# The last MLP's first matrix as seven block products, with weight sums made by adding DMAs

## The chip, the cores and the metric

The kernel runs on one core of a Trainium2 chip. The metric is the device time of one execution in microseconds; before the change the median of three runs is 2379.36 us (2377.18 to 2381.88).

## What is computed

A trunk of two layers on 1024 tokens of width 1024. Layer 0 is an mLSTM mixer and an MLP, layer 1 a latent attention mixer and an MLP. What matters here is the MLP, which both layers have:

```python
D_MODEL, SEQ, D_FF = 1024, 1024, 4096

def sqrelu_mlp(h, w1, w2):
    return jnp.square(jax.nn.relu(h @ w1)) @ w2

for l in range(DEPTH):
    ...
    x = x + g1[:, None, :] * rmsnorm(y, norm_g[l, 1])
    h = modulate(rmsnorm(x, norm_g[l, 2]), sh2, sc2)
    y = sqrelu_mlp(h, mlp_w1[l], mlp_w2[l])
    x = x + g2[:, None, :] * rmsnorm(y, norm_g[l, 3])
```

## The kernel before

**Halves.** The 1024 tokens are worked on as two halves of 512 (`hfs[0]`, `hfs[1]`). Activations lie with features on the 128 partitions and tokens along the free dimension, in 8 blocks of 128 x 512 for a half.

**Three matmuls for one product.** Each operand is split into a high part (fp32r) and the rest (low, fp32r), and `mm3` (L230 to L233) adds low x high, high x low and high x high. So a 128 x 128 block of weights against 512 tokens is three matmuls of 512 columns. A weight tile of 128 x 1024 is loaded by `wload` into one of four `raw` buffers (L211, SP's queue), and `wsplit` makes its two parts in the `ws` buffers, of which there are eight: a cast on ScalarE (L189) and a subtraction on VectorE (L190).

**The MLP.** `mlp` (L946) is a generator of steps. `hidden(f)` makes one block of 128 hidden features for 512 tokens: 8 blocks of D x 3 matmuls = 24 matmuls of 512 columns into one PSUM bank `ps`, then relu and square on ScalarE (L962, L963) and the split into high and low (L471, L472). `up_rows` and `up_cols` multiply a group of hidden blocks (4 in the last MLP) by a part of the second matrix, again 24 matmuls a step, and add the result to the output tiles (`accumulate`, L198). Hidden steps and up steps alternate: the ups of one group stand between the hidden steps of the next. Each step's weights are asked for two steps ahead (`AHEAD`, L944). There are four MLPs of 64 such steps: layer 0 half 0, layer 0 half 1, layer 1 half 0, layer 1 half 1, in this order.

**The order of the work.** Python generators are woven by hand. `two_streams` steps an MLP as the dense stream beside another stream (a mixer of the other half), and a filler. `go` ties the PE instructions of a step behind the last PE instruction before it; instructions of other engines are not tied by it, and each engine's order comes from a scheduler that takes an instruction when its operands and buffers are there. The first MLP (`f0`) runs beside a filler (`bg_latent`) that loads the adaLN weights (L352), makes the rotary tables (L1078 to L1102) and folds weights. The second and third MLPs run beside the mixers of layer 1. The last one runs beside `all_out`, which turns the residual stream into rows (`x_to_rows`, L1573 to L1579) and writes the output (`rows_out`, L1611 to L1623): the first half's in the middle of the last MLP, the second half's at its end.

**Norm before the MLP.** `post` adds the mixer's output to the residual, takes the norm and calls `normed`, which writes the split `h2`: 8 multiplications by gain and norm (L481) and 8 splits with a shift (L474 on ScalarE, L475 on VectorE).

**POOL.** GpSimd does little: nine small loads at the start (L264), the memset of the gate weights (L613), of the value tiles (L645, L648), small memsets that claim a buffer (L170), and in attention one memset for each even block (L1346).

Of the kernel before, what the change touches and what calls it, by code (L numbers as in the profile page):

```python
# [9 lines left out]
F32 = mybir.dt.float32  # L10
# [7 lines left out]
P = 128  # L18
# [64 lines left out]
def kernel(  # L83
# [39 lines left out]
    def k4v(dt=F32, b=512):  # L123
        return k4(dt)[:, :1024].rearrange("p (a b) -> p a b", b=b)
# [13 lines left out]
    def tmc(dt=F32):  # L138
        return sb.tile([P, 512], dt, tag="tmc", bufs=TMC, name=f"tmc_{next(uid)}")
# [42 lines left out]
    def paced():  # L182

        return tc.issue_after(pace[0]) if pace[0] else nullcontext()
# [42 lines left out]

    pe_last = [None]

    def mm3(o, lh, ll, rh, rl, start, stop):  # L230
        nc.tensor.matmul(o, ll, rh, start=start, stop=False)  # L231
        nc.tensor.matmul(o, lh, rl, start=False, stop=False)  # L232
        pe_last[0] = nc.tensor.matmul(o, lh, rh, start=False, stop=stop)  # L233


    nc.scalar.preload_act_table_set("natural_log_exp_and_others")
# [231 lines left out]
    def split_mod(hi, lo, u, sh):  # L468

        if sh is None:  # L470
            nc.scalar.copy(hi, u)  # L471
            nc.vector.tensor_sub(lo, u, hi.bitcast(F32))  # L472
        else:
            nc.scalar.activation(hi, u, AF.Identity, bias=sh)  # L474
            nc.vector.scalar_tensor_tensor(lo, u, sh, hi.bitcast(F32), ALU.add, ALU.subtract)  # L475

    def normed(h, xs_, rstd, A, sh):

        for k in range(KD):
            with paced():  # L480
                nc.vector.scalar_tensor_tensor(  # L481
                    xs_[k], xs_[k], A[:, k : k + 1], rstd, ALU.mult, ALU.mult
                )
                split_mod(h.hi[k], h.lo[k], xs_[k], sh[:, k : k + 1])
            if k % 4 == 3:
                yield 1

# [455 lines left out]
    NF = DFF // P  # L943
    AHEAD = 2  # L944

    def mlp(l, hf, y, sizes, rows=False):  # L946


        w1, w2, h = mlp_w1[l], mlp_w2[l], hf.h2
        hids = {}  # L950

        def hidden(f):
            def hid(w):
# [99 lines left out]
        for G in sizes:  # L1053
            fs = list(range(f0, f0 + G))
            f0, done = f0 + G, 0
            for i in range(G):
# [7 lines left out]
        for n in range(len(steps) + AHEAD):  # L1064
            if n < len(steps):
                ready.append(steps[n][0]())
            if n >= AHEAD:
                yield from steps[n - AHEAD][1](ready.pop(0))

                yield steps[(n - AHEAD + 1) % len(steps)][1].__name__  # L1070


    rope_d = scratch([2, P, S], "rope_d")
# [494 lines left out]

    def x_to_rows(half):

        for k in range(KD):
            a, b = tmc(), tmc()
            nc.sync.dma_start(a, xs_blk(k, half))  # L1573
            yield
            pt = pc()
            for t in range(4):
                nc.tensor.transpose(pt[:, ts(t, P)], a[:, ts(t, P)], ident)
            nc.scalar.copy(b, pt)
# [19 lines left out]
    def rows_out(hf, y, B):  # L1598

        xt = []  # L1600
        for t in range(4):
            a = k4v()
            r0 = hf.i * H + t * P
            nc.sync.dma_start(a, xr[r0 : r0 + P, :].rearrange("p (a b) -> p a b", b=512))
            xt.append(a)
        yield
        for t in range(4):
            yt, st = y.t[t], small(4)
            for g in range(2):
                junk = ps()  # L1610
                nc.scalar.activation(junk, yt[:, g], AF.Square, accum_out=st[:, g : g + 1])  # L1611
            ys = [tmc(), tmc()]
            v, r, w = small(1), small(1), small(1)
            with tc.high_priority(PRIO):
                for g in range(2):
                    nc.vector.tensor_mul(ys[g], yt[:, g], B[:, g])
                nc.vector.tensor_scalar(v, st[:, 0:1], st[:, 1:2], 1.0 / D, ALU.add, ALU.mult)
                nc.vector.tensor_scalar_add(v, v, EPS)
                rsqrt_(r, v, w)
            for g in range(2):  # L1620
                nc.vector.scalar_tensor_tensor(ys[g], ys[g], r, xt[t][:, g], ALU.mult, ALU.add)
                r0 = hf.i * H + t * P
                nc.sync.dma_start(out[0, r0 : r0 + P, ts(g, 512)], ys[g])  # L1623
            yield


# [126 lines left out]
    A1 = gain(2, NG(0, 2), adac(0, SC2))  # L1753
    B1 = gate(3, NG(0, 3), adac(0, G2))

    def post(hf, y, B, src, A, sh):
# [5 lines left out]
        yield 0  # L1762
        hf.h2 = Split()
        yield from normed(hf.h2, y, rstd, A, sh)

# [124 lines left out]
    drain(p1)  # L1890
    two_streams(f0, behind(bg_latent(), 4))
    rope_perm()


    z1 = FH(claim=True)
    ya = [None, None]

    def mixer1(hf, z, attention):
        att = attention(hf)
        lat = latent(hf, lambda: next(att))  # L1900
        next(lat)

        yield from to_x(hf, z)
        yield "fill"
        yield from lat
        yield next(att)
        yield from att
# [6 lines left out]
        yield from post(hf, y, B2, x_cols, A3, adac(1, SH2))  # L1914
# [5 lines left out]
    two_streams(mlp(1, hfs[0], u0, [2] * 16, True), mixer1(hfs[1], z1, attention_second))  # L1920
    u1 = FH(claim=True)

    def all_out():
        yield from x_to_rows(0)
# [43 lines left out]
```

## Time and profile before

| | |
|---|---|
| profiled execution | 2377.5 us |
| its span | 2375.5 us |
| median of the runs | 2379.36 us |
| granted TensorE clock, mean | 0.997 |
| instructions | 30534 |
| loads of MLP weights | 256 of 512 KB |

The page's times are of one execution. Matmuls are pipelined: a matmul's printed duration is longer than the distance to the next one's start, and the distance is what a row of matmuls costs. A group's line gives its count, its busy time, the mean duration in ns, then the idle time of the engine before it and what ended that. In a window's answer the columns are the busy times of PE, PEld (weight loads), DVE, ACT and POOL with their counts, the clock, the share of the DMA engines in use and GB/s.

### The profile page before, as it was taken

What the parts mean: (1) busy time and instruction counts of PE and PEld (TensorE: products, weight loads), DVE (VectorE), ACT (ScalarE), POOL (GpSimd) and SP (SyncE); (2) the same over time, 40 slices, a digit from 0 to 9 for tenths busy, and PEclk for the clock granted to TensorE, in tenths of its full rate; (3) what the DMA queues carried; (4) which work ended last, traced back from release to release, by engine and by line L of the source; (5) the groups of instructions that cost most, each with busy time, mean ns of one, the idle gap of its engine ahead of it and who ended that gap; (6) DMA issues with size and microseconds to landing.
All of it is one profiled execution on the core that took longest, in us unless ns stands there. A gap on an engine that the chain in (4) does not pass through costs nothing.

```text
span 2375.5 us, 30534 instructions
## 1 busy us (share of the span) xinstructions
PE 2343.4 (99%) x11621; PEld 1946.7 (82%) x11621; DVE 1549.6 (65%) x2435; ACT 1055.6 (44%) x1716; POOL 18.2 (1%) x93
## 2 busy tenths in 40 slices
PE   7999999999999999999999999999999999999998
PEld 5888888788888888888888888888888888888887
DVE  6667866868666667877764967765666486353345
ACT  4355334655333454434443554444444453444333
POOL 1000000000000000000000000000000000000000
PEclk9999999999999999999999999999999999999999
DMA  9452664544664745555543454874434354364431
GB/s 313 149 142 85 186 181 139 168 133 144 186 181 143 250 135 187 160 161 183 182 133 113 147 166 163 249 248 136 148 98 143 114 169 129 102 191 140 144 102 62
DMA packets 377106, 374.48 MB, mean 158 GB/s; under 512 B 24355, under 2 KB 282464, under 8 KB 376960
## 3 DMA queue, kind: packets, MB, share of 16 engines
q1 hardware_dynamic: 376672, 372.44, 50.3%
q8 instruction: 91, 1.49, 0.3%
q14 instruction: 55, 0.45, 0.1%
q0 software_dynamic: 288, 0.10, 0.0%
HBM read 313.24 MB, written 59.24 MB: 157 GB/s over the span
## 4 chain that ended last, share of the span: by engine, by line
PE 89%; DVE 4%; DMA 4%; ACT 1%; issue 1%; SPq 0%; DVEq 0%; ACTq 0%
PE ps L231 16%; PE ps L233 16%; PE ps L232 16%; PE pm L231 9%; PE pm L232 9%; PE pm L233 9%; PE pc L1450 1%; DMA raw<-in_a_w_in_dram 1%; DMA raw<-in_mlp_w_dram 1%; PE pc L231 1%; PE pc L233 1%; PE pc L232 1%; PE pm L1336 1%; DVE wl L190 1%; PE pm L820 1%
## 5 line engine op out<-in xcount | busy, mean ns | idle before, releaser
L190 DVE TENSOR_TENSOR wl<-raw,wh 128x1024 fp32r<-128x1024 f32 (+2 forms) x366 | 438.9, 1202 | 442.7 <-ACT wh L189 435.7
L189 ACT CAST wh<-raw 128x1024 fp32r<-128x1024 f32 (+2 forms) x366 | 377.6, 1035 | 704.3 <-PE ps L231 381.7
L231 PE MATMUL ps<-k,wl 128*128 128x512 f32 x1528 | 605.2, 396 | 2.5 <-ACT k L679 1.4
L233 PE MATMUL ps<-k,wh 128*128 128x512 f32 x1528 | 596.1, 390 | 0.0
L232 PE MATMUL ps<-k,wh 128*128 128x512 f32 x1528 | 595.6, 390 | 0.0
L231 PEld LDWEIGHTS ps<-k,wl 128*128 128x128 f32 x1528 | 287.0, 188 | 65.1 <-issue 2.9
L233 PEld LDWEIGHTS ps<-k,wh 128*128 128x128 f32 x1528 | 286.8, 188 | 61.7 <-issue 0.5
L232 PEld LDWEIGHTS ps<-k,wh 128*128 128x128 f32 x1528 | 287.2, 188 | 58.8 <-issue 1.7
L198 DVE TENSOR_TENSOR k<-k,pm 128x512 f32<-128x512 f32 (+1 forms) x254 | 211.0, 860 | 104.1 <-PE pm L233 103.6
L231 PE MATMUL pm<-hd,wl 128*128 128x512 f32 x512 | 200.9, 392 | 0.5 <-ACT hd L471 0.5
L232 PE MATMUL pm<-hd,wh 128*128 128x512 f32 x512 | 199.3, 390 | 0.2 <-DVE hd L472 0.2
L233 PE MATMUL pm<-hd,wh 128*128 128x512 f32 x512 | 199.2, 389 | 0.0
L231 PE MATMUL pm<-wh,hd 128*128 128x512 f32 x488 | 192.2, 394 | 1.6 <-ACT raw L1342 1.3
L232 PE MATMUL pm<-wl,hd 128*128 128x512 f32 x488 | 190.9, 391 | 0.0
L233 PE MATMUL pm<-wh,hd 128*128 128x512 f32 x488 | 190.2, 390 | 0.0
L359 DVE SCALAR_TENSOR_TENSOR tma<-raw,cond,tma 128x512 f32<-128x512 f32 x168 | 125.6, 748 | 20.4 <-DMA raw<-in_kv_ada_w_dram 14.4
L472 DVE TENSOR_TENSOR hd<-tmp,hd 128x512 fp32r<-128x512 f32 x128 | 88.3, 690 | 54.7 <-ACT hd L471 54.4
L1342 ACT ACTIVATE raw<-pm,sm 128x128 f32<-128x128 f32 (+3 forms) x64 | 47.5, 742 | 150.1 <-DVE sm L1341 121.8
L231 PEld LDWEIGHTS pm<-hd,wl 128*128 128x128 f32 x512 | 96.2, 188 | 20.8 <-ACT hd L471 0.9
L232 PEld LDWEIGHTS pm<-hd,wh 128*128 128x128 f32 x512 | 96.1, 188 | 20.5 <-DVE hd L472 0.5
L233 PEld LDWEIGHTS pm<-hd,wh 128*128 128x128 f32 x512 | 96.1, 188 | 20.2
L231 PEld LDWEIGHTS pm<-wh,hd 128*128 128x128 f32 x488 | 91.6, 188 | 22.3 <-ACT raw L1342 3.5
(354 smaller groups left out, 3426.2 us busy)
## 6 DMA issues: line engine op xcount, KB each, us to landing
raw<-in_mlp_w_dram SPq DMA_DIRECT2D x256, 512.0 KB, 4.2
raw<-in_ada_w_dram SPq DMA_DIRECT2D x80, 512.0 KB, 4.2
raw<-in_a_w_in_dram SPq DMA_DIRECT2D x48, 512.0 KB, 4.8
xs<-k SPq DMA_DIRECT2D x40, 256.0 KB, 4.8
raw<-in_kv_ada_w_dram SPq DMA_DIRECT2D x16, 512.0 KB, 4.0
raw<-in_a_w_out_dram SPq DMA_DIRECT2D x16, 512.0 KB, 4.8
kd<-k SPq DMA_DIRECT2D x32, 256.0 KB, 3.8
vd<-k SPq DMA_DIRECT2D x32, 256.0 KB, 4.5
```

The lines of the kernel that those rows point to most:

```text
L189: nc.scalar.copy(hi[:, :n], r[:, :n])
L190: i = nc.vector.tensor_sub(lo[:, :n], r[:, :n], hi[:, :n].bitcast(F32))
L198: return f(*a, **k)
L231: nc.tensor.matmul(o, ll, rh, start=start, stop=False)
L232: nc.tensor.matmul(o, lh, rl, start=False, stop=False)
L233: pe_last[0] = nc.tensor.matmul(o, lh, rh, start=False, stop=stop)
L359: nc.vector.scalar_tensor_tensor(acc, r[:, kk], cond[:, k : k + 1], acc, ALU.mult, ALU.add)
L472: nc.vector.tensor_sub(lo, u, hi.bitcast(F32))
L820: nc.tensor.matmul(nv[:, r, i], hf.PT[p_][:, r, cs], v[2 * p_ + r], start=g == 0, stop=True,)
L1336: nc.tensor.matmul(o[:, :w], qh, kh, start=False, stop=True)
L1342: nc.scalar.activation(pr[:, :n], f, AF.Exp, bias=m, scale=SCALE, accum_out=l)
L1450: nc.tensor.transpose(pt[:, ts(2 * e + i, P)], u.prs[i][:, ts(b + e, P)], ident)
```

## The change

The last MLP (layer 1, half 1) makes its hidden blocks in pairs. The 1024 rows of a pair's weights are cut in two (kh), its 256 hidden features in two (even, odd), the 512 tokens in two, and the four result blocks are made from seven block products of 512 x 128 x 256 in place of eight, by sums of operand blocks:

- **Operands of tokens.** `quarters` takes the place of the split `h2` for this half: seven quarter-size sums (`B[1]` to `B[7]`), each split into high and low. Four are made when the norm is, three at step 61 of the MLP before (`with_rest`).
- **Operands of weights.** `weight_sums` makes four sums for each of 16 pairs in a DRAM scratch `sums`: eight DMAs of 128 x 4 x 128 fp32 (256 KB) on POOL's queue, four that copy and four that add to what is there. One group of them is issued after each yield of the first MLP. The other three weight blocks are read from the weights as they are.
- **Steps.** A pair has four steps with 2, 2, 1 and 2 products of 12 matmuls of 256 columns. The banks go on accumulating after ScalarE or VectorE have taken a partial result (`more=True`). Up steps stand behind the first and the second. Loads are asked for three steps ahead.
- **Output.** `x_to_rows` loads the next block of x while it turns one; `rows_out` asks for x one row tile at first, then up to three; `all_out` goes one step at every second step of the MLP. The claim of `u1` is gone.

```diff
+    def weight_sums(w):
+        for p_ in range(NF // 2):
+            a = lambda f, kh: wcols(w, (2 * p_ + f) * P, P, 4 * kh, 4)
+            o = lambda i: by_k(sums[p_][:, ts(i, H)])
+            put = nc.gpsimd.dma_start
+            put(o(1), a(1, 0))
+            put(o(2), a(1, 0))
+            yield
+            put(o(1), a(0, 0), accum_op=ALU.add)
+            put(o(2), a(1, 1), accum_op=ALU.add)
+            yield
+            put(o(0), o(1))
+            yield
+            put(o(0), a(1, 1), accum_op=ALU.add)
+            yield
+            put(o(3), o(0))
+            yield
+            put(o(3), a(0, 1), accum_op=ALU.add)
+            yield
...
+            def product(i, o, w, start=False):
+                (wh, wl), (bh, bl) = w, B[i]
+                for k in range(4):
+                    mm3(o, wh[:, k], wl[:, k], bh[k], bl[k], start and k == 0, k == 3, more=not start)
...
+            def first(w):
+                u.b, u.x, u.s, u.r = cut(ps()), cut(pc()), tmp(), tmp()
+                product(1, u.b, w[0], True)
+                    nc.scalar.copy(u.s1, u.b)
+                product(2, u.x, w[1], True)
+                    nc.vector.tensor_add(c, u.s1, u.x)
+                    nc.scalar.activation(c, c, AF.Relu)
...
+            def second(w):
+                u.z = cut(pc())
+                product(6, u.b, w[0])
+                    nc.scalar.copy(u.s16, u.b)
+                product(7, u.z, w[1], True)
+                    nc.scalar.copy(u.s7, u.z)
...
+            def third(w):
+                u.w3 = w[1]
+                product(5, u.b, w[0])
+                    nc.vector.tensor_add(u.r[:, N:], u.s7, u.b)
...
+            def fourth(w):
+                product(4, u.z, w)
+                    nc.vector.tensor_add(cut(u.r), u.s16, u.z)
+                    nc.scalar.activation(u.r, u.r, AF.Relu, scale=-1.0)
+                    finish(2 * p_ + 1, u.r)
+                product(3, u.b, u.w3)
+                    nc.scalar.activation(u.s[:, N:], u.b, AF.Relu)
+                    finish(2 * p_, u.s)
...
+                (lambda: pieces(wload([(0, 0, wcols(w1, 2 * p_ * P))], P)), first),
+                (from_sums(0), second),
+                (from_sums(1), third),
+                (lambda: wload([(0, 0, wcols(w1, (2 * p_ + 1) * P, P, 4, 4))], P), fourth),
...
+            for i in range(0, G if B else 0, 2):
+                four = pair(fs[i] // 2)
+                for part in (four[:1], four[1:2], four[2:]):
+                    steps += part
+                    if part is not four[2:] and done < len(prev):
+                        steps.append(up(prev, done, False))
+                        done += 1
...
+        early = AHEAD + bool(B)
...
+    def with_weight_sums(g):
+        bg = weight_sums(mlp_w1[1])
+        for v in g:
+            next(bg, None)
+            yield v
+        drain(bg)
...
-    two_streams(f0, behind(bg_latent(), 4))
+    two_streams(with_weight_sums(f0), behind(bg_latent(), 4))
...
-    dense = mlp(1, hfs[1], u1, [4] * 8, True)
+    dense = mlp(1, hfs[1], u1, [4] * 8, True, B)
+    n = 0
     while (d := go(dense)) is not end:
-        if v != "last" and d != "within":
+        n += d != "within"
+        if v != "last" and d != "within" and n % 2:
             v = next(fill)
```

`finish` squares a hidden block on ScalarE and splits it, as the hidden step did.

More of the change, by code (lines that the diff above doesn't have):

```diff
@@ L1762, in post @@
         yield 0
+        if kept:
+            yield from kept(y, rstd)
+            return
         hf.h2 = Split()
@@ L1890, with quarters, part, rest @@
     drain(p1)
-    two_streams(f0, behind(bg_latent(), 4))
+    two_streams(with_weight_sums(f0), behind(bg_latent(), 4))
     rope_perm()
+    B = {}
+    later = [None]
+    def quarters(y, rstd):
+        q = lambda kh, th, j: y.t[2 * kh + j][:, :, ts(th, 256)]
+        sub = nc.vector.tensor_sub
+        def part(i, kh, th):
+            t = [k4v(F32R, 256), k4v(F32R, 256)]
+            for j in range(2):
+                s = ts(j, 2)
+                split_wide(t[0][:, s], t[1][:, s], q(kh, th, j))
+            B[i] = [[a[:, k] for k in range(4)] for a in t]
+        yield from normed_kept(y, rstd, A3, adac(1, SH2))
+        part(1, 0, 0)
+        part(2, 1, 0)
+        yield 1
+        minus = lambda o, a: nc.vector.scalar_tensor_tensor(
+            o, a, -1.0, o, ALU.mult, ALU.subtract
+        )
+        for j in range(2):
+            sub(q(0, 0, j), q(0, 0, j), q(0, 1, j))
+        part(3, 1, 1)
+        for j in range(2):
+            sub(q(0, 1, j), q(1, 1, j), q(0, 1, j))
+            minus(q(1, 1, j), q(0, 0, j))
+        part(6, 1, 1)
+        for j in range(2):
+            minus(q(1, 0, j), q(1, 1, j))
+        def rest():
+            part(7, 0, 1)
+            part(5, 0, 0)
+            part(4, 1, 0)
+        later[0] = rest
+        yield 1
     z1 = FH(claim=True)
@@ L1913, in mixer1, with with_rest @@
         yield 1
-        yield from post(hf, y, B2, x_cols, A3, adac(1, SH2))
+        yield from post(hf, y, B2, x_cols, A3, adac(1, SH2), quarters if hf.i else None)
     two_streams(mlp(0, hfs[1], z1, [2] * 14 + [4]), mixer1(hfs[0], z0, attention_first), bg_rest())
     u0 = FH(claim=True)
-    two_streams(mlp(1, hfs[0], u0, [2] * 16, True), mixer1(hfs[1], z1, attention_second))
-    u1 = FH(claim=True)
+    def with_rest(g):
+        n = 0
+        for v in g:
+            if v != "within":
+                n += 1
+                if n == 61:
+                    later[0]()
+            yield v
+    two_streams(
+        with_rest(mlp(1, hfs[0], u0, [2] * 16, True)), mixer1(hfs[1], z1, attention_second)
+    )
+    u1 = FH()
     def all_out():
```

97 lines of the change are left out of this document (78 added, 19 removed).

## The prediction

> **What bounds the kernel now.** I read the page's busy times and its chain first, then the windows, then single stages.
>
> ```profile
> PE 2343.4 (99%) x11621; PEld 1946.7 (82%) x11621; DVE 1549.6 (65%) x2435; ACT 1055.6 (44%) x1716; POOL 18.2 (1%) x93
> ...
> PE 89%; DVE 4%; DMA 4%; ACT 1%; issue 1%; SPq 0%; DVEq 0%; ACTq 0%
> ```
>
> TensorE is busy for 99% of the span and is 89% of the chain that ended last: only work taken from PE, or PE made to wait, can move the end. The windows (PE, PEld, DVE, ACT and POOL busy, clock, DMA share, GB/s) show where PE isn't full.
>
> ```profile
> 0.00:10.00 10.00, 3.17 (x10) 1.55 (x10) 3.99 (x21) 5.50 (x9) 6.21 (x22) 1.00 0.77 272
> 10.00:20.00 10.00, 8.43 (x45) 5.78 (x44) 5.86 (x12) 6.70 (x14) 0.00 (x0) 1.00 1.05 385
> 20.00:30.00 10.00, 6.12 (x28) 3.18 (x27) 7.52 (x14) 4.41 (x7) 0.00 (x0) 0.70 1.06 375
> 30.00:40.00 10.00, 10.00 (x54) 6.70 (x53) 8.39 (x14) 1.71 (x3) 0.00 (x0) 0.96 1.06 386
> ```
> ```profile
> 2010.87:2365.60 354.73, 354.73 (x1584) 292.65 (x1583) 154.02 (x217) 143.34 (x221) 0.00 (x0) 1.00 0.40 123
> ```
>
> The first 40 us are bound by loads: DMA share 1.05 at 385 GB/s, PE with gaps. The last MLP (2010.87 to 2365.6) is the other extreme: PE never idle, DVE 43%, ACT 40%, DMA 0.40. The change edits the second place; its weight sums may land in the first.
>
> **The products.** The MLP's first matrix today is 24 matmuls of 512 columns per hidden block of 128; the change makes it 84 of 256 columns for two blocks (7 products x 4 k x 3). The rate is the distance between starts, not the printed duration, since matmuls overlap. One hidden step, first matmul to the first of the next:
>
> ```profile
> 2010.87 0.39 PE L231 MATMUL ps<-k,wl 128*128 128x512 f32 x1
> ...
> 2016.31 0.39 PE L231 MATMUL ps<-k,wl 128*128 128x512 f32 x1
> ```
>
> 24 starts in 5.44 us: 0.2267 us each. For 256 columns with new weights each time, the value projection of layer 0:
>
> ```profile
> 303.48 0.28 PE L233 MATMUL ps<-wh,k 128*128 128x256 f32 x1
> ...
> 305.99 0.28 PE L233 MATMUL ps<-wh,k 128*128 128x256 f32 x1
> ```
>
> 21 starts (7 triples) in 2.51 us: 0.1195 us each, 5% more than half of 0.2267. Before: 32 x 24 x 0.2267 = 174.1 us. After: 16 x 84 x 0.1195 = 160.6 us. **-13.5 us**, not the eighth of 174 (21.8) that seven products for eight suggest. The Trainium skill (TensorE: Matmul & The Clock Gate, "Back-to-back issue gap") gives N/2.4 + 2.5 ns, an estimate of 109 ns for 256 columns and 216 for 512; by it the gain would be 19 us. The trace disagrees by 10 us per thousand matmuls at both sizes, and the trace is used.
>
> **What the products add.** Durations of the last MLP, then of 256-column forms elsewhere:
>
> ```profile
> L190 DVE TENSOR_TENSOR wl<-raw,wh 128x1024 fp32r<-128x1024 f32 x61 | 74.6, 1223 | 151.4 <-ACT wh L189 151.2
> ...
> L472 DVE TENSOR_TENSOR hd<-tmp,hd 128x512 fp32r<-128x512 f32 x32 | 22.1, 692 | 17.5 <-ACT hd L471 17.5
> ```
> ```profile
> L189 ACT CAST wh<-raw 128x1024 fp32r<-128x1024 f32 x61 | 64.3, 1054 | 169.9 <-PE ps L231 142.8 <-PE pm L232 27.1
> L963 ACT ACTIVATE tmp<-tmp 128x512 f32<-128x512 f32 x32 | 20.3, 635 | 1.0
> L471 ACT CAST hd<-tmp 128x512 fp32r<-128x512 f32 x32 | 19.8, 620 | 1.0
> L962 ACT ACTIVATE tmp<-ps 128x512 f32<-128x512 f32 x32 | 18.9, 590 | 0.0
> ```
> ```profile
> L1470 ACT COPY tmp<-ps 128x256 f32<-128x256 f32 x24 | 9.0, 373 | 11.5 <-PE ps L233 11.4
> ```
> ```profile
> L472 DVE TENSOR_TENSOR k<-ps,k 128x256 fp32r<-128x256 f32 x8 | 3.4, 421 | 0.8 <-ACT k L471 0.8
> ```
>
> - Load: a pair needs 3.5 loads of 512 KB in place of 2. DVE gets 24 more splits (29 us) and 48 adds of 0.42 (20): 203 of some 345 us. ACT gets 24 casts (25) and 48 copies of 0.37 (18): 187. DMA goes from 64 such loads to 88, share 0.40 to 0.55. None is near PE. The loads three ahead cover it: four raw tiles hold four steps. The one slot that comes late (the third step's second weights live until the fourth ends) makes an ACT cast wait, with the fourth step's relu and square behind it; they are needed a step of 24 x 0.1195 = 2.9 us later, so 0.
> - Waits of PE: product 3 goes into the bank that DVE has just added from; product 4 covers 12 x 0.1195 = 1.43 us. The add takes 0.42, and 1.64 if a weight split is ahead of it: 0 to 0.2 us, 16 times. I take **+1** of 0 to 3.4; the other banks have a whole second-matrix step between writer and reader.
> - The end: today an up step (5.4 us) stands between the last hidden step and the closing steps. After, the fourth step is followed by them at once. From product 3's end: relu 0.37, square 0.635, cast 0.62, subtract 0.69 = 2.3, and about 0.8 more because ACT is still on the odd block's three (1.85 us, begun 0.42 after product 4, against product 3's 1.43). The closing step's first six matmuls (1.36) use the earlier pair. **+2** (0 to 3).
> - New groups: seven per pair in place of two, 80 more group starts. No such row stands alone; 0 to 0.05 us each, **+1**.
>
> **The four-quarter operands.** Eight DVE operations of 0.75 go, 14 splits and 8 sums come: about +9 us on DVE, +9 on ACT, in the MLP before.
>
> ```profile
> L475 DVE SCALAR_TENSOR_TENSOR k<-k,ada,k x8: 748/751/753, 1953.3 to 1965.8; 128x512 fp32r<-128x512 f32 x8
> ```
>
> The old operands were ready at 1966.5, and PE came to them at 2010.87: 44 us of cover. The last three quarters are made at step 61 of 64, 16 us before the end of that MLP, and product 7 comes third. Cost 0; if that cover were gone, 9. The output steps of the first half go at every second step, and their loads of x move on SP's queue from four at once to one, then two: behind them stand weight loads. Of 24 k4 tiles the quarters hold 14, two results 8, a gain 1, so one is free, and an x load can keep SP until DVE has finished a tile's rows. The weight load behind it is three steps early, so 0 (to 3). The memset claim dropped on POOL costs and gains nothing.
>
> **The weight sums.** 128 DMAs of 256 KB on POOL's queue, half copies, half adding, 33.5 MB written. No row shows an adding DMA, or one from DRAM to DRAM. What POOL pays to issue, and the nearest transfers:
>
> ```profile
> L264 POOL DMA_DIRECT2D raw<-in_ada_b_dram x2 | 1.1, 542 | 0.0
> L264 POOL DMA_DIRECT2D raw<-in_norm_g_dram x1 | 0.7, 705 | 0.3 <-issue 0.3
> ...
> L264 POOL DMA_DIRECT2D raw<-in_a_gate_b_dram x1 | 0.5, 502 | 0.0
> ```
> ```profile
> DMA packets 66022, 61.62 MB, mean 175 GB/s; under 512 B 4048, under 2 KB 54736, under 8 KB 66001
> ...
> q1 hardware_dynamic: 66001, 61.35, 56.4%
> ```
>
> Two rows of data cost 0.50 us to issue, 64 rows of 512 bytes 0.70: 3.3 ns per row, so 512 runs cost between 0.5 and 2.2 us. All 128: 64 to 282 us of POOL, which is otherwise busy for 18. In the first MLP (512 to 865 us, the second fence) 61.35 MB took 56.4% of 353 us, 308 GB/s; 33.5 MB are 109 us at that rate, up to twice that if adding reads the old sum as well. Spread there the share becomes 0.87 to 1.18, with loads two steps (10.9 us) ahead. So where do they run? They wait for nothing but each other. What the trace does with such work:
>
> ```profile
> L1078 SPq DMA_DIRECT2D inv<-in_inv_freq_dram x4: 311/699/2118, 28.8 to 34.2; - x4
> ```
> ```profile
> L1081 DVE MEMSET sg<- x4: 59/59/59, 2.4 to 2.7; 32x1 f32 x4
> ```
> ```profile
> L1085 SPq DMA_DIRECT2D tmc<-in_positions_dram x2: 420/497/574, 538.8 to 572.5; - x2
> ```
>
> All three are written in the filler of the first MLP. The third needs a shared buffer and runs there; the first two need none and run in the first 35 us. The sums' DRAM has no other user either, so at least their first copies can start at some 7 us, in the stretch bound by loads. Against a large price: six of a pair's eight wait for an earlier one of the pair to land, and after 40 us PE is full and loads have slack. I take **+2** in the forecast (0 to 5), and the rest as rivals.
>
> **Sum.** -13.5 + 1 + 2 + 1 + 2 = -7.5 us. The profiled execution took 2377.5 us, 1.9 below the median 2379.4; so 2370.0 there and **2372** as a median. Its own range: 2366 (all extras 0) to 2379.
>
> **Rivals.**
> 1. *The sums crowd the start.* From 8 to 35 us loads set the pace. POOL issuing every 2.2 us puts 12 DMAs there, 3.2 MB; at 385 GB/s that is 8 us later for everything. At 0.5 us it would be 54, 14 MB and 37 us. I price it at 13, near the dearer issue, which is for the longer form: 2372 - 2 + 13 = 2383, and 2407 at worst. For it: inv and sg. Against it: most of the chain has to wait for landings. The Trainium skill (DMA: Bandwidth & Descriptors, "Queues, rings and completion order") says that each engine takes turns between the queues it has work for, packet by packet; by that rule the loads could lose no more than half, so 27 us at most: 2397.
> 2. *POOL's queue comes late (slower).* One mechanism, one place: memsets stand in POOL's queue behind DMAs that were put ahead of them.
>
> ```profile
> L613 POOL MEMSET raw<- x2: 955/956/956, 47.4 to 155.1; 128x1024 f32 x2
> ```
> ```profile
> L626 PEld LDWEIGHTS ps<-k,raw x8: 187/188/188, 78.4 to 81.6; 128*128 128x128 f32 x8
> ```
>
> The gate weights' memset runs at 47.4, and PE needs it by 78.4. It decides from (78 - 7) / 2.2 = 32 DMAs ahead of it at the dear issue, 142 at the cheap one. With 64 ahead at 1.35 us, the middle, POOL is 7 + 86 - 78 = 15 us late and PE stands still: 2372 - 2 + 15, with rival 1's 13, is 2398. If all 128 go ahead at 2.2 it is 211 late: 2581. For it: POOL is idle and nothing else holds the sums. Against: the order of POOL's queue isn't known, and the cheap issue just fits.
> 3. *The products don't come at 0.1195.* If weights and banks make it 0.127, 7 ns more, the 1344 matmuls take 170.7 us, 3.4 less than today, and the extras eat that: 2377.5 - 3.4 + 6 + 1.9 = 2382. For it: PEld needs 188 ns per load. Against: the value projection loads new weights for each matmul at 0.1195.
>
> **Chances.** Forecast 0.43, rival 1 0.28, rival 2 0.19, rival 3 0.10. About 0.2% (4.8 us) is what a measurement of this kernel can tell. Faster (under 2374.6): most of the forecast and a little of rivals 1 and 3, 0.44. Same: part of rival 1 and of rival 3 and the forecast's upper edge, 0.22. Slower: 0.34. The range 2364 to 2400 takes in the forecast, rivals 1 and 3 and the edge of rival 2, and leaves out 0.18.
>
> **What would show it.** In the last MLP: 256-column matmuls 0.12 us apart, PE idle under 5 us, the MLP some 10 us shorter. At the start: PE's first dense matmuls still near 29 us (forecast) or near 42 (rival 1); the gate weights' memset at 47 or far later (rival 2). Where the adding DMAs lie in time, and POOL's time for one, decide between them. The forecast is wrong if PE has new idle time before 300 us, or if products start 0.127 us apart.

## The result and the profile after

The changed kernel takes 2476.94 us (median of 4 runs, 2475.88 to 2483.12) against 2379.95 for the kernel before (4 runs beside it): a ratio of 1.0414, 95% interval 1.0393 to 1.0434. It is 97 us slower, and outside the predicted range of 2364 to 2400. Its profiled execution took 2483.12 us, the longest of the four, with a span of 2481.1; so differences between the two profiled spans (105.6 us) come out some 9 us larger than those of the medians.

The busy rows, the slices and the chain of the page after:

```profile
PE 2358.3 (95%) x12197; PEld 1976.7 (80%) x12197; DVE 1603.4 (65%) x2529; ACT 1098.0 (44%) x1826; POOL 139.9 (6%) x217
...
PE   3976999999999999999999999999999999999997
...
POOL 6454000000000000000000000000000000000000
PEclk6888999999999999999999999999999999999999
DMA  9999446454455575555445545674432553556552
...
PE 10%; DVE 2%; ACT 1%; issue 1%; DVEq 0%; ACTq 0%
```

PE fell from 99% to 95% of a longer span. One slice is 62 us: the loss stands in the first four, where POOL's digits are 6, 4, 5 and 4, the DMA engines are full and the clock that PE is granted is below full. (The chain's shares add up to 14%: followed back from the end it breaks off early, so it isn't used here.) The first 40 us, to be held against the windows of before:

```profile
0.00:10.00 10.00, 2.77 (x9) 1.48 (x10) 4.00 (x21) 5.09 (x9) 7.53 (x22) 1.00 0.79 272
10.00:20.00 10.00, 7.38 (x32) 5.75 (x32) 1.94 (x6) 7.53 (x14) 6.93 (x14) 1.00 1.06 314
20.00:30.00 10.00, 0.47 (x4) 0.28 (x3) 0.00 (x0) 0.58 (x1) 5.24 (x8) 0.67 1.04 322
30.00:40.00 10.00, 1.92 (x4) 0.22 (x4) 1.76 (x3) 0.00 (x0) 5.83 (x8) 0.50 1.03 351
```

PE has 2.4 us of work between 20 and 40 us where it had 16.1, at the same DMA share. What the DMA engines carry instead are the sums. POOL's issues, by four of the sums' lines (ns shortest/median/longest, first and last start), then the gate weights' memset (line 629 after, 613 before):

```profile
L973 POOL DMA_DIRECT2D sums<-in_mlp_w_dram x16: 741/741/812, 8.1 to 46.4; - x16
L976 POOL DMA_DIRECT2D sums<-in_mlp_w_dram x16: 1245/1245/2220, 48.3 to 127.2; - x16
L979 POOL DMA_DIRECT2D sums<-sums x16: 523/523/583, 130.3 to 151.8; - x16
...
L985 POOL DMA_DIRECT2D sums<-in_mlp_w_dram x16: 1245/1287/3829, 209.7 to 238.3; - x16
```
```profile
L629 POOL MEMSET raw<- x2: 952/1208/1463, 102.9 to 240.2; 128x1024 f32 x2
```

All 128 were put at the front of the program, level by level over all pairs: the 32 first copies (line 973 and its twin 974), which wait for nothing, from 8 us on, and everything else behind them until 240 us. The first memset comes at 102.9 in place of 47.4, the second at 240.2 in place of 155.1. In the first 60 us the queues and landings are, of after:

```profile
q0 software_dynamic: 3793, 8.97, 51.2%
q1 hardware_dynamic: 5528, 10.17, 50.3%
...
sums<-in_mlp_w_dram POOLq DMA_DIRECT2D x40, 256.0 KB, 10.1
...
k<-in_ada_w_dram SPq DMA_DIRECT2D x8, 512.0 KB, 29.5
```

and of before:

```profile
q1 hardware_dynamic: 12389, 18.51, 89.6%
...
k<-in_ada_w_dram SPq DMA_DIRECT2D x8, 512.0 KB, 10.6
```

The loads moved 10.17 MB where they had moved 18.51; the eight early loads of this row land after 29.5 us (median), not 10.6. PE waits for them (engine and line, what it waits for: total us, times, longest):

```profile
PE pc L321 <- DMA k<-in_ada_w_dram: 31.6, 4, 15.6
```

and the first dense matmul, before and after, is this one:

```profile
29.39 0.80 PE L231 MATMUL pm<-k,wl 128*128 128x512 f32 x1
```
```profile
69.72 0.80 PE L232 MATMUL pm<-k,wl 128*128 128x512 f32 x1
```

It is 40 us late. (Both are 0.80 us long where later ones take 0.39: in both kernels PE comes to it out of waits.) The first claim ahead of the second output projection shows the whole delay of the start:

```profile
413.50 0.10 POOL L170 MEMSET k<- 128x1 f32 x1 [195.55 <-DVE hd L791]
```
```profile
499.83 0.10 POOL L170 MEMSET k<- 128x1 f32 x1 [195.53 <-DVE hd L807]
```

That is 86.3 us, from before to after. The second 46 of them aren't loads alone. By PE's waits of after up to 320 us, 14.0 us go to the gate arithmetic on DVE and ACT (L727, L741, L743), for which PE doesn't wait in before. Another 12.6 and 6.9 us go to work behind ACT's casts, and between 195 and 245 us these casts wait 19.9 us for weight loads. The same 14.0 us stand in e3, e5 and e11 below. The other loss is at the other end. The last MLP of after, as one window:

```profile
2104.37:2473.00 368.63, 350.92 (x2181) 313.54 (x2179) 201.27 (x300) 181.57 (x324) 0.00 (x0) 1.00 0.51 160
```

PE idles 18 us in it, and from first to last matmul it takes 367.1 us (2104.37 to 2471.45) where it took 355.7 (2010.87 to 2366.57): 11.4 more, not 7.5 less. The matmuls themselves are as forecast:

```profile
2104.37 0.28 PE L232 MATMUL ps<-k,wl 128*128 128x256 f32 x1
...
2108.56 0.28 PE L234 MATMUL pc<-k,wh 128*128 128x256 f32 x1
```

35 distances of starts in 4.19 us, 0.1197 each. What PE waits for there:

```profile
PE pm L232 <- DVE hd L473: 12.3, 8, 2.7
PE ps L232 <- DVE tmp L1046: 2.8, 6, 1.5
PE ps L232 <- ACT tmc L1034: 1.5, 2, 0.7
```

Eight times a second-matrix step stands in front of a hidden block that DVE hasn't split yet. Counted by the distance of starts beyond 0.1195 or 0.2267 us, which holds the restart as well, the last MLP's gaps are 24.6 us: 14.4 of that kind, 4.1 of the second, 1.9 of the third, and 4 in small pieces. The products did bring their part: 1344 of them at 0.1197 us are 160.9 us, against 174.1 before, 13.2 us less.

### The profile page after: what moved, and what is told of

It reads as the page before. It is cut to its first block, busy times and chain, and to the rows that moved or that the text cites. A ratio compares the mean times of both kernels' runs of the same rounds, so it can differ in the third digit from the quotient of the medians.

```text
span 2481.1 us, 32203 instructions
## 1 busy us (share of the span) xinstructions
PE 2358.3 (95%) x12197; PEld 1976.7 (80%) x12197; DVE 1603.4 (65%) x2529; ACT 1098.0 (44%) x1826; POOL 139.9 (6%) x217
## 3 DMA queue, kind: packets, MB, share of 16 engines
q0 software_dynamic: 39200, 33.66, 7.5%
## 5 line engine op out<-in xcount | busy, mean ns | idle before, releaser
L190 DVE TENSOR_TENSOR wl<-raw,wh 128x1024 fp32r<-128x1024 f32 (+3 forms) x398 | 469.4, 1182 | 397.4 <-ACT wh L189 390.6
L189 ACT CAST wh<-raw 128x1024 fp32r<-128x1024 f32 (+3 forms) x398 | 403.7, 1018 | 634.6 <-PE ps L232 234.8
L232 PE MATMUL ps<-k,wl 128*128 128x512 f32 (+1 forms) x1528 | 580.0, 380 | 26.2 <-ACT hd L695 12.6
L234 PE MATMUL ps<-k,wh 128*128 128x512 f32 (+1 forms) x1528 | 571.0, 374 | 0.0
L233 PE MATMUL ps<-k,wh 128*128 128x512 f32 (+1 forms) x1528 | 570.3, 373 | 0.0
L232 PE MATMUL pm<-wh,hd 128*128 128x512 f32 x488 | 194.2, 398 | 14.7 <-DVE hd L473 12.3
L232 PEld LDWEIGHTS pm<-wh,hd 128*128 128x128 f32 x488 | 92.0, 188 | 38.7 <-DVE hd L473 16.1
L473 DVE TENSOR_TENSOR hd<-tmp,hd 128x512 fp32r<-128x512 f32 x128 | 87.6, 688 | 38.3 <-ACT hd L472 37.2
```

Of the source, the lines that this page charges most:

```text
L189: nc.scalar.copy(hi[:, :n], r[:, :n])
L190: i = nc.vector.tensor_sub(lo[:, :n], r[:, :n], hi[:, :n].bitcast(F32))
L232: nc.tensor.matmul(o, ll, rh, start=start, stop=False, **m)
L233: nc.tensor.matmul(o, lh, rl, start=False, stop=False, **m)
```

## The experiments

Theory A: the sums cost the 86 us, by taking DMA time from loads at the start; the last MLP loses 11 us to the order of its steps. Its rivals (B to I) stand with the runs. Ratios are to the kernel before, run on the same chip; a run without an interval was timed once.

| run | us | ratio, 95% | first claim | last MLP |
|---|---|---|---|---|
| before | 2377 to 2380 | 1 | 413.50 | 355.7 |
| after | 2476.94 | 1.0393 to 1.0434 | 499.83 | 367.1 |
| e1_held | 2439.49 | 1.0248 to 1.0279 | 415.02 | 365.6 |
| e2_no_sums | 2388.99 | 1.0038 to 1.0068 | 413.03 | 367.1 |
| e3_sums_alone | 2463.09 | | 498.80 | as before |
| e4_held_order | 2428.22 | 1.0201 to 1.0236 | 413.39 | 357.5 |
| e5_dve_memsets | 2476.39 | | 496.05 | 368.5 |
| e6_paced | 2411.67 | 1.0127 to 1.0155 | 412.34 | 366.9 |
| e7_paced_guard | 2414.59 | 1.0136 to 1.0167 | 414.35 | 370.4 |
| e8_paced_order | 2391.35 | 1.0042 to 1.0067 | 413.91 | 348.9 |
| e9_dve_sums | 2372.07 | 0.9969 to 0.9987 | 413.42 | 350.3 |
| e10_thin | 2385.82 | 1.0021 to 1.0049 | 411.45 | 350.8 |
| e11_copies | 2455.29 | | 491.41 | as before |
| e12_order_no_sums | 2372.53 | 0.9965 to 0.9984 | 413.95 | 350.5 |

"First claim" is POOL's memset shown above, "last MLP" the time from its first to its last matmul.

### The sums, away and alone

**e3_sums_alone**: the kernel before with the generator of the sums (the one of the change) run beside its first MLP, and nobody reading them. 

> The kernel before with the 128 sum DMAs added and read by nobody: the last MLP is today's. Theory A: the start alone is late, by 80 to 90 us, and the last MLP takes 355 us: 2455 to 2470. Rival C: below 2420, since the start is then late by something else of the change.

**e2_no_sums**: the change with

```
-    wload([(0, 0, by_k(sums[p_][:, 2 * i * H : 2 * (i + 1) * H]))], P)
+    wload([(0, 0, by_k(w2[(2 * p_ + i) * P : (2 * p_ + i + 1) * P, :]))], P)
...
-    two_streams(with_weight_sums(f0), behind(bg_latent(), 4))
+    two_streams(f0, behind(bg_latent(), 4))
```

> Left out: the weight sums are neither made nor read; the steps that read them read rows of the second matrix of the same size and shape instead, so the products are not the reference's. All else is the change. Theory A: the same as with the sums held, 2390 to 2397, since they are free there; what remains over before is the last MLP (+12) and the middle (+5 to 7). Rival B: 20 us or more below the kernel with the sums held. Rival D (the first MLP's order, not the sums, holds the middle's loss): the middle is late here too.

The two halves add up. The sums alone cost 85.9 us (2463.09 against 2377.16), all of it before the first claim; the change without them costs 11.8 (2388.99), nearly all of it in the last MLP; together 97.7, and the change costs 97.0. Rival C (the start is late for something else) is out. The middle of e2 and of e3 isn't late; the 7 us that the profile of after loses there are about what its execution lies above the other three.

### The sums, later

**e1_held**: each sum DMA is queued on POOL behind the claim of the first MLP's result.

```
-            next(bg, None)
+            with tc.issue_after(z0.claimed):
+                next(bg, None)
...
-        drain(bg)
+        with tc.issue_after(z0.claimed):
+            drain(bg)
```

> All 128 sum DMAs are queued on POOL behind the claims of the first MLP's result (557 us in before); the rest is the change as it is. Theory A (at the start the sums cost 86 us, by holding up loads and POOL's memsets; in the first MLP they are free, since the DMA queues are 56% busy there): the start is as before (second out-projection's claim near 413 us, not 500), the sums lie between 557 and 850 us, the middle stays some 7 us late and the last MLP at 367 us: profiled span near 2394, median 2397 (2390 to 2402), 1.007 of before. Rival B (33.5 MB cost the same wherever they run, as loads and sums share the queues): PE gains idle time between 557 and 850 us, 20 to 80 us of it: 2415 to 2475. Rival C (the start is late for another reason than the sums, such as another order of the whole program): the claim stays near 500 us and the time near 2477.

The start is as before (415.02), but the time is 50.5 us over e2. My expectation of free sums fell; rival B was right in sign. The sums ran from 450.7 to 704 us, not from 557 as expected. Up to 520 us they cost nothing (PE is busy all the time in both kernels), and from 520 to 560 little (38.84 of 40 us), in a stretch where the loads of before have a DMA share of 0.36 to 0.51; nearly the whole loss comes after it. The windows of e1_held from 560 us on, where before has PE at 40.00 of 40 and a DMA share of 0.52 to 0.64:

```profile
560.00:600.00 40.00, 33.98 (x126) 27.23 (x127) 29.10 (x42) 19.07 (x26) 20.65 (x24) 0.83 1.15 260
600.00:640.00 40.00, 31.16 (x124) 24.52 (x122) 30.12 (x45) 13.70 (x18) 18.39 (x21) 0.91 1.22 262
```

and the queues of 560 to 720 us with the landing of the weight loads, e1_held and then before:

```profile
q0 software_dynamic: 22444, 17.89, 64.7%
q1 hardware_dynamic: 21580, 21.79, 46.8%
...
raw<-in_mlp_w_dram SPq DMA_DIRECT2D x21, 512.0 KB, 11.7
```
```profile
q1 hardware_dynamic: 30191, 27.53, 56.9%
...
raw<-in_mlp_w_dram SPq DMA_DIRECT2D x29, 512.0 KB, 4.5
```

The loads run two steps (10.9 us) ahead; they land after 11.7 us in place of 4.5, and then have a cast and a split to come. So PE waits for weights, as e1's rows of 560 to 720 us show (after the last bar, idle time and what ended it):

```profile
L232 PE MATMUL ps<-k,wl 128*128 128x512 f32 x80 | 38.1, 477 | 25.0 <-DVE wl L190 25.0
...
L189 ACT CAST wh<-raw 128x1024 fp32r<-128x1024 f32 x21 | 22.0, 1047 | 92.3 <-DMA raw<-in_mlp_w_dram 89.6 <-PE pm L232 2.6
```

In the windows with these waits the clock granted to PE is lower too (0.83 and 0.91).

**e6_paced**: four sum DMAs behind each of the 32 memsets that POOL does for the attentions, level by level over all pairs.

```
-            nc.gpsimd.memset(pr[:, n : n + P], 0.0)
+            with tc.issue_after(nc.gpsimd.memset(pr[:, n : n + P], 0.0).ins):
+                for _ in range(4):
+                    next(bg_sums, None)
```

> The sums are spread: four of the 128 DMAs behind each of POOL's 32 memsets in the two attentions (962 to 1807 us of before), all pairs level by level, so that each one's source has long landed. The rest is the change. Theory A2 (the sums cost PE time only where they run back to back, as loads then get half of the DMA time; spread over 850 us they add 0.1 to the queues' share and cost 0 to 5 us): start and first MLP as in before, the last MLP still 367 us, the whole 2386 to 2394, as without sums (2389). Rival B (each MB of the sums costs PE about the same wherever it runs, 50 us in the first MLP): PE gains 20 to 50 us of waits in the attentions: 2405 to 2440.

0.9% (21 us) over e2: less than half of the 50, but not free. The time lies in rival B's range; theory A2 fell as I had put it. By name, PE's waits are mostly not on loads here (the longest rows are 5.4 us on ACT's L1482 and 5.2 on DVE's L473), and four adding DMAs keep POOL for some 5 us, in which a memset of the attention can stand behind them; so part of the 21 us may be POOL's. That wasn't run apart.

**e10_thin**: one sum DMA at a time, on the reordered steps of e8 below.

```
+        if nth[0] is not None:
+            nth[0] += 1
+            if nth[0] % 2 == 0:
+                m = nc.gpsimd.tensor_copy(seen, lo[:, :1].bitcast(F32))
+                with tc.issue_after(m.ins):
+                    next(bg_sums, None)
```

> The reordered steps with the sums in DRAM, but one sum DMA at a time: behind every second weight tile that is split between 560 and 2000 us, POOL reads one column of that tile and issues one DMA, some 12 us apart. Theory A2 (what costs PE time is several sum DMAs in a row in front of a load; one at a time a load is late by 2 us at most, and loads are ahead by more): the 22 us that the sums behind the attentions' memsets cost fall to 0 to 6: 2370 to 2378. Rival B (the cost goes with the bytes): 15 to 25 us stay: 2385 to 2396.

**e12_order_no_sums**: e8 without sums, the base for e8 and e10. 

> Left out: the sums are neither made nor read; rows of the second matrix of the same size and shape are read in their place, so the products are not the reference's. The steps are the reordered ones. This is the base for the price of the sums wherever they are put. Theory A (order of steps and price of the sums add up): the run without sums, less the 18 us by which the reordered steps shortened the last MLP: 2369 to 2373. So spread sums cost 20 us, thinly spread ones 14, and DVE's own sums 0 to 2. Theory I (without sums the reordering gives less, as its gain came from somewhere else): 2376 or more.

2372.53, as theory A has it; rival I is out.

By the ratios, e10 is 0.6% or 14 us over e12, and e8, with the sums as in e6, 0.8% or 19 us. So 128 DMAs of 33.5 MB cost 86 us at the start, 50 in one go from 451 us on, 19 to 21 in groups of four, 14 one by one. e10's 2385.82 is in B's range, and A2 is out; but B's same cost wherever they run is out as well. Spread sums cost less and aren't free. How much of that is the spacing isn't shown, since the place changed with it: the loads of before have a DMA share of 0.57 from 560 to 720 us and of 0.51 from 960 to 1810. In e10 the loads land after 4.6 us against 4.3 in e12, and PE's waits between 560 and 2010 us add up to 15.2 against 6.7; these are 8.5 of the 14 us, and where the rest is stays open.

### What of the start is POOL's, what is the queues'

**e5_dve_memsets**: `nc.gpsimd.memset` becomes `nc.vector.memset` in the gate weights (line 629) and the value tiles' ones (661 and 664). 

> The change as it is, sums at the start included, but the three memsets of the first two projections (the gate weights', and the ones of the value tiles) run on DVE, so that no work of PE waits for POOL's queue there. Theory A1 (most of the 86 us at the start is loads that share the DMA queues with the sums): the claim of the second out-projection stays at 470 to 495 us (500 in the change, 413.5 in before), the whole at 2450 to 2475. Rival 2 of the prediction (POOL's queue comes late, and that is what PE waits for): the claim falls below 450 us, the whole below 2430.

2476.39, and the claim at 496.05, both just past the upper end of A1: POOL's late memsets carry at most 4 of the 86 us (the time is 0.55 us below the median of the change). They come late, as rival 2 of the prediction said, but PE is itself late by then.

**e11_copies**: e3 with `accum_op=ALU.add` taken out of the four adding lines. 

> The kernel before with 128 DMAs at the start as in the run with the sums alone (read by nobody), but each a plain copy, none adding; so what is written are no sums. Theory R (a DMA that adds costs the queues what a copy costs): 75 to 86 us at the start, as with the sums: 2453 to 2464. Rival S (an adding DMA costs about twice a copy, as it reads the old sum too, and POOL 1.25 us in place of 0.74): 50 to 65 us: 2427 to 2443.

The queue of the sums between 0 and 260 us, with adding DMAs (e3) and with copies (e11):

```profile
q0 software_dynamic: 39200, 33.66, 71.3%
```
```profile
q0 software_dynamic: 10528, 33.66, 39.0%
```

The same 33.66 MB take 185 us of all 16 engines in one and 101 in the other (71.3% and 39.0% of 260), 1.8 times. But only half of e3's DMAs add, so an adding one costs more than that. In e10 32 copies stand alone between 560 and 905 us, and 32 adding DMAs between 905 and 1325:

```profile
q0 software_dynamic: 2560, 8.39, 7.3%
```
```profile
q0 software_dynamic: 16896, 8.39, 19.9%
```

That is 25 us of all 16 engines for 8.39 MB copied and 84 for as much added: 3.3 times, in 528 packets a DMA and not 80. (In e6, where four run in a row, the same working gives 29 and 71 us, 2.4 times.) Rival S was right that adding costs more, and too low; yet theory R's time came true, for a reason that neither held: copies are issued faster, so more of them stand in the stretch that loads bound. By 69.44 us e11 has issued 51 DMAs from the weights (12.23 MB moved on POOL's queue), e3 43 (9.58 MB), and e11's loads have moved 10.92 MB, e3's 12.24. The first dense matmul of e3 and of e11:

```profile
69.44 0.80 PE L231 MATMUL pm<-k,wl 128*128 128x512 f32 x1
```
```profile
80.36 0.80 PE L231 MATMUL pm<-k,wl 128*128 128x512 f32 x1
```

51 us late with copies, 40 with adds. From there to the claim it is the other way round: 27 us more with copies (78 in all), 45 with adds (85). PE's longest wait of that part in e3, 11.4 us on L679 behind late casts, isn't in e11.

### The last MLP's steps

**e4_held_order**: e1 with product 4 moved from the fourth step to the third, whose second weights are then product 4's own, and the second-matrix steps behind the second and third step.

```
             def third(w):
-                u.w3 = w[1]
                 product(5, u.b, w[0])
...
+                product(4, u.z, w[1])
...
             def fourth(w):
-                product(4, u.z, w)
-                product(3, u.b, u.w3)
+                product(3, u.b, w)
...
-                for part in (four[:1], four[1:2], four[2:]):
+                for part in (four[:2], four[2:3], four[3:]):
```

> The sums held as in the first run, and the last MLP's steps put in another order: product 4 moves to the third step (its weights are loaded with product 5's), the fourth step is product 3 alone, and the two second-matrix steps of a pair follow the second and the third step, not the first and the second. So no weights are held over a step, and 48 matmuls (5.7 us), not 24 (2.9 us), stand between a group's last hidden block and its first reader. Theory A (PE's 24 us of waits in the last MLP are mostly that reader, late behind ACT casts that wait for a held slot, and product 3 behind its bank's add): the waits fall to 5 to 9 us, the MLP takes 348 to 353 us, some 15 to 18 less than with the sums held alone: median 2377 to 2384. Rival E (the waits move: copies and adds between the first and second step, or loads, are now late): the last MLP stays over 360, and the time within 6 us of the run with the sums held alone.

357.5, 8 us better than e1, between the two theories. PE waits for one hidden block (2.2 us) where it waited for eight (12.3). The whole is only 11 us below e1, far above theory A's 2377 to 2384, which took the held sums as free. PE's timeline showed why: second-matrix steps came three to the first pair of a group and one to the second. The list of steps has the guard `part is not four[2:]`, in the change as in my edit; a slice is a new object each time, so the guard always holds. My reading of the change, in which each pair had two, was wrong.

**e7_paced_guard**: e6 with that guard mended (`j < 2`, with `j` counted over the parts), nothing else. 

> The sums spread as in the run before, and one condition in the list of steps mended: the change compares a slice with a freshly made slice, which is never the same object, so a third second-matrix step follows the first pair of a group and the second pair has one where two were meant. Now each pair has two. Theory F (product 3's wait for the add in its bank, 4 to 6 us in all, comes from the pair whose third and fourth step follow the second without cover; the 14 us at the borders of groups stay, since a second-matrix step still comes 24 matmuls behind the last hidden block): the last MLP 361 to 364 us, the time 3 to 6 us below the spread run. Rival G (uneven steps are also what makes the border late): the waits on the hidden blocks go too, 349 to 354 us, 13 to 18 below.

Wrong in both versions: 370.4, 3.5 us more than e6. PE's waits of e7 in the last MLP:

```profile
PE pm L232 <- DVE hd L473: 10.1, 7, 2.2
PE ps L232 <- DVE tmp L1054: 6.9, 12, 1.5
```

With two steps for each pair, none stands between a pair's third and fourth step any more, and product 3 waits for the add in its bank twelve times instead of six (line 1054 is 1046 of the change).

**e8_paced_order**: e7 and e4 together. 

> The sums spread, each pair given two second-matrix steps, behind its second and third step, product 4 in the third step and product 3 alone in the fourth, so that no weights are held over a step. Theory A: PE's waits in the last MLP fall from 24 to 4 to 8 us, the MLP takes 346 to 350 us: 16 to 21 below the spread run, 2368 to 2375, 0.996 to 0.999 of before. Rival E (what is left of the waits moves: copies between a pair's first and second step, the closing steps, loads): 355 us or more, 2377 or more, no faster than before.

348.9, inside the 346 to 350. Of the waits, of e8, this is left:

```profile
PE pm L232 <- DVE hd L473: 2.1, 1, 2.1
PE ps L232 <- ACT tmc L1042: 1.5, 2, 0.7
```

The 20 us below e6 came as expected too; the whole time was expected too low, at 2368 to 2375, as that took the sums for free.

**e9_dve_sums**: the steps of e8, and no sums in DRAM: DVE adds them in SBUF, in place, from the pair's two weight tiles.

```
+            def load2():
...
+                for to, b in ((f1, f0), (f0, f1)):
+                    add(u.A[:, f0], u.A[:, f0], u.B[:, b])
+                    split_wide(hi[:, to], lo[:, to], u.A[:, f0])
...
+            def load3():
+                add(u.B[:, f0], u.B[:, f0], u.B[:, f1])
...
+            def load4():
+                add(u.A[:, f1], u.A[:, f1], u.A[:, f0])
```

> No sums in DRAM at all: in the last MLP DVE makes the four weight sums in place from a pair's two weight tiles, just before each is split (four additions of 128x512, about 0.69 us each, so 2.8 us of DVE a pair, 44 in all, and the loads of the pair fall from 3.5 to 2). The steps stand as in the run with the sums spread and the steps reordered. Theory A (the sums' cost was the DMA queues', the last MLP's was the order of its steps): start and middle as in the kernel before, the last MLP 348 to 353 us against 355.7, so 2368 to 2374, 0.996 to 0.999 of before. Rival H (DVE, then busy for some 250 of 350 us, delays the splits of the hidden blocks, or two weight tiles held through a pair starve the loads): PE gains 8 us or more of waits in the last MLP: 2378 or more.

2372.07 (11 runs), 0.9969 to 0.9987 of the kernel before, and the same as e12, in which no sums are made at all (though e12 loads 3.5 tiles a pair, and e9 two). Rival H is out; the window of its last MLP:

```profile
2004.00:2352.00 348.00, 344.12 (x2171) 310.68 (x2169) 235.21 (x364) 183.16 (x331) 0.00 (x0) 1.00 0.42 134
```

DVE is busy for 68%, the DMA share is 0.42, and PE idles 4 us. This version beats both kernels, by 0.2% and 4.2%.

## Why the prediction was wrong

- **The products** were right: 0.1197 us a start, and 13.2 us of the 13.5; rival 3 is out. The estimate by the Trainium skill's formula (TensorE: Matmul & The Clock Gate, "Back-to-back issue gap") was 19; the trace's own rate held.
- **Where the sums run** is the step that failed first. The rows of inv and sg said that work that waits for nothing runs at the front; the forecast set against it that six of a pair's eight DMAs wait for a landing. It didn't count what was left: two of eight in 16 pairs are 32 DMAs and 8 MB that wait for nothing, in a stretch bound by loads. +2 was taken, 86 measured.
- **Rival 1** had the mechanism and mis-sized it twice. It was priced at 13 us "near the dearer issue" of 2.2 us; a copy took POOL 0.74, and the cheap end, 54 DMAs and 37 us, was the nearer one: 40 DMAs by 60 us, 40 us late. And "after 40 us PE is full and loads have slack", the forecast's argument against it, was wrong: another 46 us followed by the claim, and in e1, where PE was full and loads were two steps ahead, the sums still cost 50. There the first 109 us of the sums were nearly free, and the loss came after 560 us, at the same DMA share (1.07 to 1.24 up to 680 us). Whether the loads' lead was used up by then, or their own higher share after 560 us did it, isn't shown.
- **Turns between queues.** In the first 60 us the two queues had 51.2% and 50.3% of the engines. That agrees with the turns of which the Trainium skill tells (DMA: Bandwidth & Descriptors, "Queues, rings and completion order"). The bound that I drew from it, 27 us, didn't hold (40). It took half of the engines for half of the bytes: from 30 to 69.72 us the loads moved 6.66 MB, 168 GB/s, where before had 375 to 386 in all. And PE ran slower between its waits, at a granted clock of 0.50 from 30 to 40 us. The Trainium skill (TensorE: Matmul & The Clock Gate, "What's actually happening") says that PE drops to half rate after some 3.4 us without work. The trace agrees on the half; the 3.4 us no view here shows.
- **DMA cost of adding**: the 109 us of engine time for all 33.5 MB, "up to twice that" with adding, were right for the sum (101 for copies alone, 185 with half of them adding). An adding DMA by itself was dearer, 2.4 to 3.3 times a copy.
- **Rival 2** saw the memsets late and blamed them. They were (102.9 and 240.2), but e5 puts at most 4 us to them.
- **The loads three ahead, "so 0"**, is the step that failed in the last MLP: 14.4 us. Its own numbers spoke against it: the working gave PE a step of 2.9 us there, and, two items further on, 3.1 us for the chain from product 3 to the split block. And it dismissed the cast that waits for the held slot because what is behind it isn't needed at once. One such event, in the timeline of after:

```profile
2125.89 1.05 ACT L189 CAST wh<-raw 128x1024 fp32r<-128x1024 f32 x1 [2.22 <-PE pc L232]
...
2126.84 0.63 ACT L1060 ACTIVATE tmp<-tmp 128x512 f32<-128x512 f32 x1
...
2127.37 1.03 ACT L189 CAST wh<-raw 128x1024 fp32r<-128x1024 f32 x1
...
2128.30 0.37 ACT L1064 ACTIVATE tmp<-ps 128x256 f32<-128x256 f32 x1
...
2129.89 0.61 ACT L472 CAST hd<-tmp 128x512 fp32r<-128x512 f32 x1
...
2130.39 1.06 ACT L189 CAST wh<-raw 128x1024 fp32r<-128x1024 f32 x1
...
2132.63 0.68 DVE L473 TENSOR_TENSOR hd<-tmp,hd 128x512 fp32r<-128x512 f32 x1
...
2133.37 0.50 PE L232 MATMUL pm<-wh,hd 128*128 128x512 f32 x1 [1.57 <-DVE hd L473]
```

  ACT stands 2.22 us before the first cast; the odd block's relu (1060) follows it, a second cast comes ahead of the even block's relu (1064), and a third ahead of its last cast; the block is ready at 2133.31, some 6 us after product 3, and PE has had 24 matmuls and six of the next step. That first cast is released by product 4, not by product 3: it gets product 4's buffer, while the held one isn't free. Without the holding, the third step's buffer would have been free when product 5 ended, some 1.5 us sooner (an estimate from the starts of the matmuls). With no slot held and 48 matmuls in between only one of these waits is left, in e4 with the uneven guard and in e8 without it (the closing one); the guard alone (e7) leaves seven. How much of that is the slot and how much the distance wasn't run apart.
- **The bank of product 3**, +1 of 0 to 3.4: 4.1 in the change, in the pairs in which no second-matrix step covers it, which the uneven guard made six. That is slightly over its bound. In the order that the forecast had in mind, two second-matrix steps a pair (e7), product 3 waits twelve times, 6.9 us: twice the bound.
- **The end**, +2: in e8 the one wait left on a hidden block, 2.1 us at 2362.73, is there. Right.
- **The quarters**, 0: in e12 the last MLP starts at 2010.64 as in before (2010.87). Right.
- **The forecast's own range** up to 2379 isn't the sum of its terms' upper bounds: 3.4 + 3 + 4 + 5 on 2379.4 - 13.5 give 2381.

So two terms failed, each for the same reason: a cost was set to nothing or next to it on the strength of a cover (landings, a step of lead) that wasn't measured against what was put under it.

## What to carry to other kernels

Work that waits for nothing is moved to where it is ready, not to where it is written: give bulk transfers something to stand behind, and before calling them hidden compare their engine time with the lead of the loads, which share the engines with them. Where a second operand can be made from tiles that are in SBUF anyway, an engine with a third of its time free is the cheaper place: DVE's sums cost nothing that could be measured, the same sums by DMA 14 to 86 us. When steps are put in a new order, follow each chain from the last product to its first reader with what stands in ACT's and DVE's queues, and read the order off the instructions, not off the loop.

## What the runs showed of the hardware

- An adding DMA from DRAM to DRAM (256 KB in 512-byte rows) took POOL 1.25 us to issue where the plain copy took 0.74 (medians of 2.0 to 3.1 in e6, four in a row). In e10 32 of them took 84 us of all 16 engines in 16896 packets, and 32 copies of the same size 25 us in 2560; in e6 it was 71 and 29 us.
- POOL's queue and SP's shared the DMA engines evenly while both had work (51.2% and 50.3%), however urgent the loads were; in e1, with adds on the one side, it was 64.7% and 46.8%.
- Late loads cost twice: the wait, and the clock. Windows with PE waiting had a granted clock of 0.50 to 0.91, and the first dense matmul after such waits took 0.80 us, later ones 0.39.
